# Retention heads: decay products ahead of the lo parts, gate weight sums in halves, and the gate's last products swapped round the first values

## The chip, the cores and the metric

The kernel runs on one core of a Trainium2 chip. The metric is the device time of one execution in microseconds (us), as a median of several executions. The engines are TensorE (PE, matmuls; PEld is its weight load), VectorE (DVE), ScalarE (ACT), GpSimd (POOL) and SyncE (SP), which issues the DMAs here. Each engine works through its own row of instructions in order and waits there for others by semaphores.

## What is computed

One decoder layer over 512 positions and 16 meta tokens at width 1024: two mixers on the same normalised input, gated retention (4 heads) and stick-breaking attention (16 heads), then an output product and a SwiGLU feed-forward part (FFN). Only retention matters for the change. Cut to that, with the chunked sums written as one:

```python
q = rotary(heads(rq)) * 256 ** -0.5      # 4 heads, 256 wide
k = rotary(heads(rk))                    # 16 meta rows ahead of the 512
v, gate = heads(rv), rg                  # 512 wide a head
scores = (q @ k.T) * decay               # decay[i, j] = g**(i-j) for i >= j, else 0
y = head_groupnorm(scores @ v)           # (y - mean) * rsqrt(var + 1e-5), per row
y_ret = (silu(gate) * y) @ w_ret_out
```

## The kernel before

**Numbers and products.** fp32 operands are carried as two parts: `split` (L99) has ACT copy a tile into the hi part, and `lo_of` (L96) has DVE subtract it from the source to give the lo part. Every product is three matmuls (hi by hi, hi by lo, lo by hi), all issued through `mm` (L90). So nearly every PE row of the profile says L90, every hi part L99 and every lo part L96, and tiles are told apart by name: `wh`/`wl` are weights' hi and lo parts, `qk` the parts of rotated q and k (later also of the transposed output), `sh`/`sl` those of the scores, `smt` those of the meta tokens' scores, `tm` a decay product, `ub` the combined results of seven products, `raw` a loaded weight, `st` a sum of weight quarters.

**Seven products.** The gate, the values and FFN multiply by a Strassen-Winograd scheme. `tok_quarters` (L255-283) loads a weight in two pieces, forms four sums of its quarters on POOL (x, y and two in place, L277-280), and splits seven units in the order a11, a12, s2, s3, s1, s4, a22. `seven` (L285-307) makes the seven products in PSUM banks and combines them on DVE into `ub` (L296, L299, L302, L307). The products are numbered 0 to 6: product 5 uses s4 and product 6 uses a22; both land in one two-bank tile. `after` is a hook in which `rv_proj` puts the meta tokens' part.

**Banks.** PSUM is handed out from three pools with two buffers each: `bank_p` (512 columns), `bank_b` (512 columns) and `bank_a` (1024 columns). Scores, y and the transposes take `bank_b`. `wraw` holds two loaded weight pieces; `rt` has three buffers for rotation temporaries, decay products and y.

**A retention head** (loop from L1045): `ret_qk` projects and rotates q, projects k in two halves of 128 rows into two `bank_a` tiles, and rotates k (`rotate`, L915-929: L921 to L923 make the first half and L925 to L928 the second, each followed by a split). `tok_quarters` loads and splits the gate's weights. `ret_scores` (L955-983) makes 6 matmuls for the meta tokens' scores, then 6 for each of four blocks j (512, 384, 256 and 128 columns), multiplies each by the decay (L966 for meta, L978 for the blocks) and splits it. `ret_gate` (L1007) makes the gate's seven products and a silu. `ret_pv` (L985) makes the four row blocks y0 to y3, each with mean, variance, reciprocal root (`rstd_of`, a power on POOL at L143) and the product with the gate; `ret_T` transposes; `rv_proj(h+1)` projects the next head's values; `ret_out` multiplies by the output weight.

**Who sets the order.** The kernel is written for a framework whose scheduler orders each engine's row. It may put instructions in another order than the code has them where their data allows, except that `keep` returns matmuls marked to keep program order while `pinned[0]` is true. In the retention heads of the kernel before it is false: the scheduler puts the gate's products between k's projection and the scores, and the scores in between them.

Of the kernel before, what the change touches and what calls it, by code (L numbers as in the profile page):

```python
# [10 lines left out]
F32 = mybir.dt.float32  # L11
# [5 lines left out]
P = 128  # L17
# [17 lines left out]
def hybrid_block(  # L35
# [219 lines left out]
    def tok_quarters(src, sums=None):  # L255

        raws = []
        for i in range(2):
            raw = wraw.tile([P, KH, 512], F32, tag="raw", name="raw")
            nc.sync.dma_start(raw, src[KH * P * i : KH * P * (i + 1), :].rearrange("(k p) c -> p k c", p=P))  # L260
            raws.append(raw)
        A11, A21 = raws[0][:, :, 0:256], raws[0][:, :, 256:]
        A12, A22 = raws[1][:, :, 0:256], raws[1][:, :, 256:]
        u = {}
        u["a11"] = wun_split(A11)
        u["a12"] = wun_split(A12)
        if sums is None:
            u["a22"] = wun_split(A22)
            nc.gpsimd.tensor_tensor(A22, A21, A22, op=ALU.add)
            nc.gpsimd.tensor_tensor(A21, A11, A21, op=ALU.subtract)  # L270
            nc.gpsimd.tensor_tensor(A11, A22, A11, op=ALU.subtract)
            nc.gpsimd.tensor_tensor(A12, A12, A11, op=ALU.subtract)
            u["s2"], u["s3"], u["s1"], u["s4"] = [wun_split(a) for a in (A11, A21, A22, A12)]
            return u
        x = sums.tile([P, KH, 256], F32, tag="st", name="st")
        y = sums.tile([P, KH, 256], F32, tag="st", name="st")
        nc.gpsimd.tensor_tensor(y, A11, A21, op=ALU.subtract)  # L277
        nc.gpsimd.tensor_tensor(A21, A21, A22, op=ALU.add)
        nc.gpsimd.tensor_tensor(x, A21, A11, op=ALU.subtract)  # L279
        nc.gpsimd.tensor_tensor(A12, A12, x, op=ALU.subtract)  # L280
        u["s2"], u["s3"], u["s1"] = wun_split(x), wun_split(y), wun_split(A21)
        u["s4"], u["a22"] = wun_split(A12), wun_split(A22)
        return u

    def seven(product, bank1, bank2, ub, after=lambda n: None):  # L285


        n = ub.shape[-1]
        p1 = bank1()
        product(0, p1)  # L290
        nc.scalar.activation(ub[:, 1, :], p1, AF.Copy)
        p = bank2()
        product(1, p[:, 0, :])
        after(1)
        product(2, p[:, 1, :])
        nc.vector.tensor_tensor(ub[:, 0:2, :], p, ub[:, 1:2, :].to_broadcast([P, 2, n]), op=ALU.add)  # L296
        p = bank1()
        product(3, p)
        nc.vector.tensor_tensor(ub[:, 2, :], p, ub[:, 1, :], op=ALU.add)  # L299
        p = bank1()  # L300
        product(4, p)
        nc.vector.tensor_tensor(ub[:, 1:4:2, :], p.rearrange("p (o n) -> p o n", o=1).to_broadcast([P, 2, n]), ub[:, 1:3, :], op=ALU.add)  # L302
        p = bank2()
        product(5, p[:, 0, :])
        product(6, p[:, 1, :])
        after(6)
        nc.vector.tensor_tensor(ub[:, 1:3, :], p, ub[:, 1:3, :], op=ALU.add)  # L307

    def feat_seven(u, tok, ub):
# [645 lines left out]
    def ret_scores(h, q, k):  # L955
        st = []
        dec = s4.tile([P, L], F32, tag="dec", name="dec", bufs=1)
        nc.sync.dma_start(dec, decay[h])
        pb = bank_b()
        n = 0  # L960
        for e in range(2):
            for a, b in ((0, 0), (0, 1), (1, 0)):
                mm(pb[:NM], k[e][a][:, 0:NM], q[e][b][:, :T], start=(n == 0), stop=(n == 5))
                n += 1
        tm = s4.tile([P, T], F32, tag="rt", name="tm", bufs=RT)
        nc.vector.tensor_tensor(tm[:NM], pb[:NM], dec[0:NM, NM:], op=ALU.mult)  # L966
        split(smt[0:16, :], smt[32:48, :], tm[:NM])
        nc.scalar.activation(smt[64:80, :], smt[0:16, :].bitcast(F32), AF.Copy)
        for j in range(NT):
            w = T - j * P  # L970
            pb = bank_b()
            n = 0
            for e in range(2):
                for a, b in ((0, 0), (0, 1), (1, 0)):
                    mm(pb[:, :w], k[e][a][:, NM + j * P : NM + (j + 1) * P], q[e][b][:, j * P : T], start=(n == 0), stop=(n == 5))
                    n += 1
            tm = s4.tile([P, T], F32, tag="rt", name="tm", bufs=RT)
            nc.vector.tensor_tensor(tm[:, :w], pb[:, :w], dec[:, :w], op=ALU.mult)  # L978
            sh = s4.tile([P, w], F32R, tag=f"sh{j}", name="sh", bufs=1)
            sl = s4.tile([P, w], F32R, tag=f"sl{j}", name="sl", bufs=1)  # L980
            split(sh, sl, tm[:, :w])
            st.append((sh, sl))
        return st

    def ret_pv(h, st, vts, us, gts):  # L985

        for i in range(NT):
            y = bank_b()
            mm(y, smt[:, i * P : (i + 1) * P], rvm, start=True, stop=False)
            for j in range(i + 1):  # L990
                cs = slice((i - j) * P, (i - j + 1) * P)
                sh, sl = st[j]
                vh, vl = vts[j]
                mm(y, sh[:, cs], vh, start=False, stop=False)
                mm(y, sh[:, cs], vl, start=False, stop=False)
                mm(y, sl[:, cs], vh, start=False, stop=(j == i))
            stt = s4.tile([P, 6], F32, tag="bn", name="bn")
            nc.vector.bn_stats(stt, y)
            mv = s4.tile([P, 2], F32, tag="mv", name="mv")
            nc.vector.bn_aggr(mv, stt)  # L1000
            rs = s4.tile([P, 1], F32, tag="rs", name="rs")
            rstd_of(rs, mv[:, 1:2], 1e-5, 1.0)
            yn = s4.tile([P, DV], F32, tag="rt", name="yn", bufs=RT)
            nc.vector.tensor_scalar(yn, y, mv[:, 0:1], rs, op0=ALU.subtract, op1=ALU.mult)
            nc.vector.tensor_tensor(gts[i], yn, gts[i], op=ALU.mult)

    def ret_gate(u):  # L1007
        ub = s4.tile([P, 4, 512], F32, tag="ub", name="ub", bufs=1)
        tok_seven(u, tokens, ub)
        g = s4.tile([P, NT, DV], F32, tag="g", name="g", bufs=1)  # L1010
        for q in range(4):
            c, t = q // 2, q % 2
            dst = g[:, 2 * t : 2 * t + 2, 256 * c : 256 * (c + 1)]
            nc.scalar.activation(dst, ub[:, q, :].rearrange("p (a b) -> p a b", a=2), AF.Silu)
        return [g[:, i, :] for i in range(NT)]

    def ret_T(gts):
        yT = []
# [27 lines left out]
    for h in range(RH):  # L1046
        q, k = ret_qk(h)
        us = tok_quarters(w_in[:, O_RG + DV * h : O_RG + DV * (h + 1)], s4)
        st = ret_scores(h, q, k)
        gts = ret_gate(us)  # L1050
        ret_pv(h, st, vts, us, gts)
        yT = ret_T(gts)
        if h + 1 < RH:
            vts = rv_proj(h + 1)
            ret_out(h, yT, first if h == 0 else add)
        else:

            gall = [s4.tile([P, 4, T], F32, tag=t, name="ga", bufs=1) for t in ("vh", "vl")]
            ga = [gall[f // 4][:, f % 4, :] for f in range(KD)]
            base = []  # L1060
            for f in range(0, KD, 2):
                mb = s4.tile([P, 2, T], F32, tag="st", name="mb")
                nc.sync.dma_start(mb, mS_d[:, f : f + 2, :])
                base += [mb[:, 0, :], mb[:, 1, :]]

                def gate(f):
                    nc.vector.tensor_tensor(acc[:, f, :], acc[:, f, :], ga[f], op=ALU.mult)
                    nc.vector.tensor_tensor(acc[:, f, :], acc[:, f, :], base[f], op=ALU.add)

                for e in range(f, f + 2):  # L1070
                    if e < NGE:
                        nc.sync.dma_start(ga[e], ga_d[:, e, :])
                    else:
                        (u,) = feat_units(w_in[:, O_GA + P * e : O_GA + P * (e + 1)])
                        ps = bank_p()
                        feat_mm(ps, u, xtok, ltok)
                        nc.scalar.activation(ga[e], ps, AF.Sigmoid)
                    gate(e)

            def merge(f, ps):  # L1080
                t = s4.tile([P, L], F32, tag="rt", name="mg", bufs=RT)[:, :T]
                nc.vector.tensor_tensor(t, ps, ga[f], op=ALU.mult)
                nc.vector.tensor_tensor(t, t, acc[:, f, :], op=ALU.add)
                split(hT[:, f, NM:], hL[:, f, NM:], t)

            ret_out(h, yT, merge)
# [225 lines left out]
```

## Time and profile before

| | us |
|---|---|
| median of 3 executions (1228.42 to 1229.15) | 1228.53 |
| the profiled execution | 1228.66 |
| its span | 1226.9 |
| mean granted TensorE clock | 0.993 |

In the span the retention heads run from about 360 to 820 us; in the four heads k's last product ends at 406.8, 515.6, 625.2 and 734.0. FFN's first products run from 875 to 1100, and its output follows to 1215. A timeline row has the start, the duration, the engine, the line, the operation, out<-in with shapes, the count, and in brackets the idle time before it with what ended that. A row by windows has start and end, the length, then the busy time and count of PE, PEld, DVE, ACT and POOL, the granted PE clock as a share of full speed, the share of the DMA engines, and GB/s.

### The profile page before, as it was taken

Reading aid. Unit: us, or ns where it says so; the run is one execution under the profiler, and the core shown is the slowest. Engines: PE = TensorE matmul, PEld = TensorE weight load, DVE = VectorE, ACT = ScalarE, POOL = GpSimd, SP = SyncE. Lnnn points to the kernel's source line nnn. Section 1 sums busy time; section 2 is a strip of 40 time slices with the busy share of each in tenths; the row PEclk is TensorE's granted clock in tenths of the full one; section 3 lists DMA queues with packets and bytes.
Section 4 is the critical chain, followed back from the end, with each engine's and each line's share of the span. In section 5 each row is a group of like instructions: output and inputs, shape, how many; then the busy total and the mean of one; then the engine's idle time right before and its main releaser. Section 6 shows DMA issues by size and latency. Waiting matters only on the chain.

```text
span 1226.9 us, 18829 instructions
## 1 busy us (share of the span) xinstructions
PE 1172.9 (96%) x7597; PEld 1063.2 (87%) x7597; DVE 884.1 (72%) x1133; ACT 532.8 (43%) x869; POOL 390.9 (32%) x425
## 2 busy tenths in 40 slices
PE   7999999889999999989999999999989999999997
PEld 7888888788889988988898899778979999998886
DVE  5588888887537885586678657776799999984333
ACT  5476666655423435342342424334354444443221
POOL 2037767553033210230212020000555666730000
PEclk9999999999999999999999999999999999999999
DMA  6331112114633213122321424424223333343211
GB/s 191 87 95 44 52 52 62 43 44 154 224 130 104 70 59 122 46 97 70 106 70 44 137 69 147 136 88 153 70 69 104 104 104 104 104 158 134 80 58 68
DMA packets 94503, 118.23 MB, mean 96 GB/s; under 512 B 2489, under 2 KB 71105, under 8 KB 94417
## 3 DMA queue, kind: packets, MB, share of 16 engines
q1 hardware_dynamic: 93984, 115.98, 29.2%
q8 instruction: 59, 0.97, 0.3%
q10 hardware_dynamic: 432, 1.07, 0.3%
q14 instruction: 28, 0.22, 0.1%
HBM read 109.96 MB, written 7.08 MB: 95 GB/s over the span
## 4 chain that ended last, share of the span: by engine, by line
PE 70%; DVE 14%; issue 4%; ACT 3%; POOL 3%; DMA 2%; DVEq 0%; POOLq 0%; ACTq 0%; SPq 0%
PE pp L90 30%; PE pb L90 18%; PE pa L90 16%; PE pc L90 4%; DVE wl L96 3%; DVE sm L645 2%; DVE sp L646 2%; PE pb L93 2%; DVE sl L96 1%; ACT wh L99 1%; POOL mg L654 1%; DMA raw<-in_w_in_dram 1%; DVE kl L96 1%; DMA raw<-in_w_sb_out_dram 1%; DMA raw<-in_w_ffn_in_dram 1%
## 5 line engine op out<-in xcount | busy, mean ns | idle before, releaser
L96 DVE TENSOR_TENSOR wl<-raw,wh 128x1024 fp32r<-128x1024 f32 (+1 forms) x202 | 275.2, 1371 | 81.1 <-ACT wh L99 77.8
L99 ACT ACTIVATE wh<-raw 128x1024 fp32r<-128x1024 f32 (+1 forms) x202 | 201.2, 1007 | 255.2 <-PE pp L90 85.5
L90 PE MATMUL pp<-hT,wh 128*128 128x512 f32 (+2 forms) x308 | 109.3, 355 | 13.0 <-DVE qb L96 8.1
L90 PE MATMUL pp<-hL,wh 128*128 128x512 f32 (+2 forms) x308 | 104.0, 338 | 0.0
L90 PE MATMUL pp<-hT,wl 128*128 128x512 f32 (+2 forms) x308 | 103.9, 337 | 0.0
L90 PE MATMUL pp<-qk,wh 128*128 128x512 f32 x256 | 83.1, 399 | 2.0 <-ACT qk L99 1.7
L96 DVE TENSOR_TENSOR wl<-st,wh 128x1024 fp32r<-128x1024 f32 x54 | 80.2, 1490 | 6.6 <-ACT wh L99 6.5
L90 PE MATMUL pp<-wh,hT 128*128 128x256 f32 (+1 forms) x240 | 78.0, 326 | 2.1 <-DVE kl L96 1.4
L90 PE MATMUL pp<-wh,hL 128*128 128x256 f32 (+1 forms) x240 | 76.6, 319 | 0.8 <-DVE ss L142 0.8
L90 PEld LDWEIGHTS pp<-hT,wh 128*128 128x128 f32 x308 | 58.6, 190 | 20.2 <-issue 10.2
L90 PE MATMUL pp<-wl,hT 128*128 128x256 f32 (+1 forms) x240 | 76.1, 317 | 0.0
L99 ACT ACTIVATE wh<-st 128x1024 fp32r<-128x1024 f32 x54 | 55.8, 1054 | 44.5 <-POOL st L279 17.1
L277 POOL TENSOR_TENSOR st<-raw 128x1024 f32<-128x1024 f32 x7 | 17.3, 2470 | 166.6 <-DMA raw<-in_w_in_dram 166.6
L143 POOL TENSOR_TENSOR rs<-rs,nhalf 128x1 f32<-128x1 f32 x20 | 12.2, 612 | 181.4 <-DVE rs L142 181.4
L654 POOL CAST mg<-sp 128x16 fp32r<-128x16 f32 x64 | 31.1, 486 | 109.4 <-DVE sp L646 53.6
L90 PEld LDWEIGHTS pp<-hT,wl 128*128 128x128 f32 x308 | 58.5, 190 | 6.1
L90 PEld LDWEIGHTS pp<-hL,wh 128*128 128x128 f32 x308 | 58.8, 191 | 3.8
L645 DVE TENSOR_TENSOR_SCAN sm<-sm,mask 128x528 f32<-128x528 f32 (+1 forms) x64 | 59.7, 946 | 2.6 <-ACT sm L641 2.1
L90 PE MATMUL pa<-hL,wh 128*128 128x264 f32 (+1 forms) x192 | 61.6, 321 | 0.0
L90 PE MATMUL pa<-hT,wl 128*128 128x264 f32 (+1 forms) x192 | 61.6, 321 | 0.0
L90 PE MATMUL pa<-hT,wh 128*128 128x264 f32 (+1 forms) x192 | 61.6, 321 | 0.0
L90 PEld LDWEIGHTS pp<-qk,wh 128*128 128x128 f32 x256 | 47.6, 188 | 13.4 <-ACT qk L99 2.4
(341 smaller groups left out, 3855.2 us busy)
## 6 DMA issues: line engine op xcount, KB each, us to landing
raw<-in_w_in_dram SPq DMA_DIRECT2D x31, 1024.0 KB, 5.0
raw<-in_w_ffn_in_dram SPq DMA_DIRECT2D x22, 1024.0 KB, 5.1
raw<-in_w_in_dram SPq DMA_DIRECT2D x26, 512.0 KB, 4.2
raw<-in_w_ffn_out_dram SPq DMA_DIRECT2D x11, 1024.0 KB, 5.0
raw<-in_w_ret_out_dram SPq DMA_DIRECT2D x8, 1024.0 KB, 5.1
raw<-in_w_sb_out_dram SPq DMA_DIRECT2D x4, 1024.0 KB, 7.4
raw<-in_w_out_dram SPq DMA_DIRECT2D x4, 1024.0 KB, 5.1
ysb<-in_x_dram SPq DMA_DIRECT2D x4, 512.0 KB, 8.9
```

Of the source, the lines that this page charges most:

```text
L90: return keep(nc.tensor.matmul(*args, **kw))
L93: return keep(nc.tensor.transpose(dst, src, idn))
L96: nc.vector.tensor_tensor(lo, src, hi.bitcast(F32), op=ALU.subtract)
L99: ins = nc.scalar.activation(hi, src, AF.Copy)
L143: nc.gpsimd.tensor_tensor(dst, dst, nhalf[:n], op=ALU.pow)
L277: nc.gpsimd.tensor_tensor(y, A11, A21, op=ALU.subtract)
L645: nc.vector.tensor_tensor_scan(rev, rev, mask[:, r0:][:, ::-1], 0.0, op0=ALU.mult, op1=ALU.max)
L646: nc.vector.tensor_tensor(sp, sp, sm[:, r0 + 1 : L + 1], op=ALU.mult)
L654: nc.gpsimd.tensor_copy(g[:, i, 0:NM], att[i][:, 0:NM])
```

## The change

There are four edits.

1. `ret_scores` issues all decay products (now L985) ahead of the blocks' splits; the meta scores' split comes at block 2, and block 3's decay product is put into the free end of block 1's `tm`.
2. `ret_gate` sets `pinned[0]` around the gate's seven products and, through the hook, puts y0's matmuls (`ret_y`) behind product 6; `ret_pv` makes y1 to y3.
3. `seven` makes product 6 ahead of product 5, wherever it is used, and `tok_quarters` splits a22 ahead of s4.
4. `tok_quarters` makes each of the four sums in two halves (the gate of each head, and the values of heads 1 to 3).

```diff
 tok_quarters:
-        nc.gpsimd.tensor_tensor(y, A11, A21, op=ALU.subtract)
-        nc.gpsimd.tensor_tensor(A21, A21, A22, op=ALU.add)
-        nc.gpsimd.tensor_tensor(x, A21, A11, op=ALU.subtract)
-        nc.gpsimd.tensor_tensor(A12, A12, x, op=ALU.subtract)
+        for d, p, q, op in ((y, A11, A21, ALU.subtract), (A21, A21, A22, ALU.add), (x, A21, A11, ALU.subtract), (A12, A12, x, ALU.subtract)):
+            for k in range(0, KH, 2):
+                nc.gpsimd.tensor_tensor(d[:, k : k + 2], p[:, k : k + 2], q[:, k : k + 2], op=op)
         u["s2"], u["s3"], u["s1"] = wun_split(x), wun_split(y), wun_split(A21)
-        u["s4"], u["a22"] = wun_split(A12), wun_split(A22)
+        u["a22"], u["s4"] = wun_split(A22), wun_split(A12)
...
 seven:
-        product(5, p[:, 0, :])
         product(6, p[:, 1, :])
         after(6)
+        product(5, p[:, 0, :])
...
 ret_scores:
-        split(smt[0:16, :], smt[32:48, :], tm[:NM])
-        nc.scalar.activation(smt[64:80, :], smt[0:16, :].bitcast(F32), AF.Copy)
+        tms = {}
         for j in range(NT):
+            if j == 2:
+                split(smt[0:16, :], smt[32:48, :], tmm[:NM])
+                nc.scalar.activation(smt[64:80, :], smt[0:16, :].bitcast(F32), AF.Copy)
...
-            tm = s4.tile([P, T], F32, tag="rt", name="tm", bufs=RT)
-            nc.vector.tensor_tensor(tm[:, :w], pb[:, :w], dec[:, :w], op=ALU.mult)
+            if j < 3:
+                tm = s4.tile([P, T], F32, tag="rt", name="tm", bufs=RT)
+                tms[j] = tm[:, :w]
+            if j == 1:
+                tms[3] = tm[:, w : w + P]
+            nc.vector.tensor_tensor(tms[j], pb[:, :w], dec[:, :w], op=ALU.mult)
+        for j in range(NT):
+            w = T - j * P
...
-            split(sh, sl, tm[:, :w])
+            split(sh, sl, tms[j])
...
 ret_gate:
+        def after(n):
+            if n == 6:
+                y0.append(ret_y(0, st, vts))
+
+        pinned[0] = True
+        tok_seven(u, tokens, ub, after=after)
+        pinned[0] = False
```

The first place is PE's row in head 0, from the last matmul of k's projection (`pa_4486`). Here `pp_4658` is the gate's first product, `qk_4409` and `qk_4410` are q's first half in hi and lo, `qk_4535` and `qk_4536` k's first half, and `pb_4593` the meta scores. Before, the gate's matmuls follow k directly, and the scores come in among them later:

```order
L90 MATMUL pa_4486<-hT_83,wl_4434 128x264
L90 MATMUL pp_4658<-wh_4557,hL_84 128x256
L90 MATMUL pp_4658<-wh_4557,hT_83 128x256
...
L90 MATMUL pa_4684<-wh_4561,hT_83 128x256
L90 MATMUL pb_4593<-qk_4409,qk_4535 16x512
L90 MATMUL pb_4593<-qk_4410,qk_4535 16x512
L90 MATMUL pb_4605<-qk_4409,qk_4535 128x512
L90 MATMUL pb_4605<-qk_4410,qk_4535 128x512
L90 MATMUL pa_4684<-wl_4562,hT_83 128x256
```

Now the scores follow k directly (`pb_4597` meta, `pb_4606` block 0; `qk_4411`, `qk_4412` are q's second half, `qk_4537`, `qk_4538` k's), and the gate's first product, `pp_4661`, comes after the last block:

```order
L90 MATMUL pa_4486<-hT_83,wl_4434 128x264
L90 MATMUL pb_4597<-qk_4409,qk_4535 16x512
L90 MATMUL pb_4597<-qk_4410,qk_4535 16x512
L90 MATMUL pb_4606<-qk_4409,qk_4535 128x512
L90 MATMUL pb_4606<-qk_4410,qk_4535 128x512
L90 MATMUL pb_4597<-qk_4409,qk_4536 16x512
L90 MATMUL pb_4606<-qk_4409,qk_4536 128x512
L90 MATMUL pb_4597<-qk_4411,qk_4537 16x512
...
L90 MATMUL pb_4636<-qk_4411,qk_4538 128x128
L90 MATMUL pp_4661<-wh_4557,hT_83 128x256
```

Between k's projection and the scores there is no matmul any more that can run without the rotated k. All four heads read alike here.

The second place is DVE's row in head 0, at the same point of the work. Before, two decay products, parts of weights (`wl`) and parts of scores (`sl`) alternate, with the fourth decay product (128 columns) behind them:

```order
L96 TENSOR_TENSOR sl_4615<-tm_4612,sh_4614 128x512
L978 TENSOR_TENSOR tm_4625<-pb_4618,dec_4591 128x384
L978 TENSOR_TENSOR tm_4638<-pb_4631,dec_4591 128x256
L96 TENSOR_TENSOR wl_4964<-raw_4957,wh_4963 128x1024
L96 TENSOR_TENSOR sl_4628<-tm_4625,sh_4627 128x384
L96 TENSOR_TENSOR sl_4641<-tm_4638,sh_4640 128x256
L978 TENSOR_TENSOR tm_4651<-pb_4644,dec_4591 128x128
L96 TENSOR_TENSOR wl_4974<-st_4967,wh_4973 128x1024
```

Now the four decay products alternate with score parts alone, and the weights' parts come behind all of them:

```order
L966 TENSOR_TENSOR tm_4604<-pb_4597,dec_4595 16x512
L985 TENSOR_TENSOR tm_4613<-pb_4606,dec_4595 128x512
L96 TENSOR_TENSOR smt_4060<-tm_4604,smt_4060 16x512
L985 TENSOR_TENSOR tm_4622<-pb_4615,dec_4595 128x384
L96 TENSOR_TENSOR sl_4645<-tm_4613,sh_4644 128x512
L985 TENSOR_TENSOR tm_4634<-pb_4627,dec_4595 128x256
L96 TENSOR_TENSOR sl_4649<-tm_4622,sh_4648 128x384
L985 TENSOR_TENSOR tm_4622<-pb_4636,dec_4595 128x128
L96 TENSOR_TENSOR sl_4653<-tm_4634,sh_4652 128x256
L96 TENSOR_TENSOR sl_4657<-tm_4622,sh_4656 128x128
L96 TENSOR_TENSOR wl_4588<-raw_4555,wh_4587 128x1024
L96 TENSOR_TENSOR wl_4592<-raw_4555,wh_4591 128x1024
```

The lo parts of the last two gate units (`wl_4588`, `wl_4592`) moved from ahead of the scores' decay products to behind the scores' last part.

More of the change, by code (lines that the diff above doesn't have):

```diff
@@ L964, in ret_scores @@
                 n += 1
-        tm = s4.tile([P, T], F32, tag="rt", name="tm", bufs=RT)
-        nc.vector.tensor_tensor(tm[:NM], pb[:NM], dec[0:NM, NM:], op=ALU.mult)
-        split(smt[0:16, :], smt[32:48, :], tm[:NM])
-        nc.scalar.activation(smt[64:80, :], smt[0:16, :].bitcast(F32), AF.Copy)
+        tmm = s4.tile([P, T], F32, tag="rt", name="tm", bufs=RT)
+        nc.vector.tensor_tensor(tmm[:NM], pb[:NM], dec[0:NM, NM:], op=ALU.mult)
+        tms = {}
         for j in range(NT):
+            if j == 2:
+                split(smt[0:16, :], smt[32:48, :], tmm[:NM])
+                nc.scalar.activation(smt[64:80, :], smt[0:16, :].bitcast(F32), AF.Copy)
             w = T - j * P
@@ L976, in ret_scores, with ret_y, ret_pv @@
                     n += 1
-            tm = s4.tile([P, T], F32, tag="rt", name="tm", bufs=RT)
-            nc.vector.tensor_tensor(tm[:, :w], pb[:, :w], dec[:, :w], op=ALU.mult)
+            if j < 3:
[6 more added lines that the diff above has]
+            w = T - j * P
             sh = s4.tile([P, w], F32R, tag=f"sh{j}", name="sh", bufs=1)
             sl = s4.tile([P, w], F32R, tag=f"sl{j}", name="sl", bufs=1)
-            split(sh, sl, tm[:, :w])
+            split(sh, sl, tms[j])
             st.append((sh, sl))
         return st
-    def ret_pv(h, st, vts, us, gts):
-        for i in range(NT):
[L988 to L996, printed above, removed]
+    def ret_y(i, st, vts):
+        y = bank_b()
+        mm(y, smt[:, i * P : (i + 1) * P], rvm, start=True, stop=False)
+        for j in range(i + 1):
+            cs = slice((i - j) * P, (i - j + 1) * P)
+            sh, sl = st[j]
+            vh, vl = vts[j]
+            mm(y, sh[:, cs], vh, start=False, stop=False)
+            mm(y, sh[:, cs], vl, start=False, stop=False)
+            mm(y, sl[:, cs], vh, start=False, stop=(j == i))
+        return y
+    def ret_pv(y0, st, vts, gts):
+        for i in range(NT):
+            y = ret_y(i, st, vts) if i else y0
             stt = s4.tile([P, 6], F32, tag="bn", name="bn")
@@ L1005, in ret_pv, with ret_gate @@
             nc.vector.tensor_tensor(gts[i], yn, gts[i], op=ALU.mult)
-    def ret_gate(u):
+    def ret_gate(u, st, vts):
         ub = s4.tile([P, 4, 512], F32, tag="ub", name="ub", bufs=1)
-        tok_seven(u, tokens, ub)
+        y0 = []
+        def after(n):
[4 more added lines that the diff above has]
+        pinned[0] = False
         g = s4.tile([P, NT, DV], F32, tag="g", name="g", bufs=1)
@@ L1014, in ret_gate @@
             nc.scalar.activation(dst, ub[:, q, :].rearrange("p (a b) -> p a b", a=2), AF.Silu)
-        return [g[:, i, :] for i in range(NT)]
+        return [g[:, i, :] for i in range(NT)], y0[0]
     def ret_T(gts):
@@ L1049, in hybrid_block @@
         st = ret_scores(h, q, k)
-        gts = ret_gate(us)
-        ret_pv(h, st, vts, us, gts)
+        gts, y0 = ret_gate(us, st, vts)
+        ret_pv(y0, st, vts, gts)
         yT = ret_T(gts)
```

## The prediction

> **What bounds the kernel now.** The page comes first. TensorE (PE) is busy for 96% of the span, so in most stages a microsecond is gained or lost only where PE waits or where its clock falls.
>
> ```profile
> span 1226.9 us, 18829 instructions
> PE 1172.9 (96%) x7597; PEld 1063.2 (87%) x7597; DVE 884.1 (72%) x1133; ACT 532.8 (43%) x869; POOL 390.9 (32%) x425
> ```
>
> The change lies mostly in the four retention heads, so the second view is PE's waits from 300 to 880 us: total, times, longest. Only two belong to the edited code, the scores' decay products and the transposed output's parts.
>
> ```profile
> PE pb L90 <- DVE tm L978: 7.6, 3, 3.2
> PE pp L90 <- ACT qk L99: 1.7, 3, 0.6
> ```
>
> The third view is a table by stretch (length; busy PE, weight loads, DVE, ACT, POOL; clock; DMA). While k of head 0 is rotated (around 407 to 414), PE is busy all the time: gate products cover the rotation. The 2.24 us wait before 432.98 is one of the three on line 978, and about 1.5 us behind it the granted clock is 0.50 for 3.41 us. Two later heads show the same.
>
> ```profile
> 400.00:430.00 30.00, 30.00 (x240) 29.20 (x239) 24.27 (x26) 12.84 (x18) 8.38 (x4) 1.00 0.22 72
> 430.74:432.98 2.24, 0.00 (x1) 0.03 (x1) 2.24 (x3) 1.12 (x3) 1.60 (x1) 1.00 0.00 0
> 434.52:437.93 3.41, 3.41 (x18) 3.41 (x18) 3.41 (x5) 0.63 (x1) 0.00 (x0) 0.50 0.11 42
> 543.75:547.16 3.41, 3.41 (x18) 3.41 (x17) 3.41 (x5) 0.77 (x2) 0.00 (x0) 0.50 0.25 74
> 652.97:656.39 3.42, 3.42 (x18) 3.42 (x17) 3.42 (x5) 0.63 (x1) 0.00 (x0) 0.50 0.16 57
> ```
>
> ```profile
> 542.74 0.47 PE L90 MATMUL pb<-rvm,smt 80*128 80x512 f32 x1 [3.17 <-DVE tm L978]
> 651.41 0.47 PE L90 MATMUL pb<-rvm,smt 80*128 80x512 f32 x1 [2.24 <-DVE tm L978]
> ```
>
> **What goes.** The fourth decay product and its lo part come late, because DVE takes weight splits and lo parts between the decay products. Now six of the gate's seven products stand between the scores and y0: 144 matmuls at 0.125 (240 in 30.00 us above), 18 us of PE work. So these waits go: 2.24 + 3.17 + 2.24 = 7.6. The clock drops that follow them should go too: each does in 3.41 us what takes 1.7 at full clock, three make 5.1. Sum removed: **12.7 us**. Head 3 has neither.
>
> **What comes: k's rotation in the open.** With the gate's products held in written order behind the scores, directly behind k's last matmul stand matmuls that need the rotated k. The timeline of DVE and ACT gives the chain (start, duration, instruction):
>
> ```profile
> 406.86 0.71 DVE L922 TENSOR_TENSOR rt<-pa,sinT 128x528 f32<-128x528 f32 x1 [3.47 <-PE pa L90]
> 407.49 0.70 DVE L926 TENSOR_TENSOR rt<-pa,sinT 128x528 f32<-128x528 f32 x1
> 408.10 0.70 DVE L923 TENSOR_TENSOR rt<-rt 128x528 f32<-128x528 f32 x1
> 408.72 1.22 DVE L96 TENSOR_TENSOR wl<-raw,wh 128x1024 fp32r<-128x1024 f32 x1
> 409.86 0.70 DVE L927 TENSOR_TENSOR rt<-pa,cosT 128x528 f32<-128x528 f32 x1
> 411.61 0.70 DVE L96 TENSOR_TENSOR qk<-rt,qk 128x528 fp32r<-128x528 f32 x1
> 412.22 0.70 DVE L928 TENSOR_TENSOR rt<-rt 128x528 f32<-128x528 f32 x1
> 413.63 0.71 DVE L96 TENSOR_TENSOR qk<-rt,qk 128x528 fp32r<-128x528 f32 x1 [0.71 <-ACT qk L99]
> ```
>
> ```profile
> 410.06 0.64 ACT L99 ACTIVATE qk<-rt 128x528 fp32r<-128x528 f32 x1
> ```
>
> Let zero be the start of L922. L923 ends at 1.94 (408.80). Before, ACT was still at two other jobs; these are no longer ahead of it, so the first hi part is done at 2.6 and PE starts at about 2.7. On DVE one weight lo part (1.22) still stands there, but the second of before is gone; stepping down the rows, which overlap by 0.08, the first lo part ends at 4.31, L928 at 4.92, ACT's second hi part at 5.6, the second lo part at 6.35.
>
> PE has 12 matmuls of 512 columns for that time (the meta tokens' scores and those of block 0), in two halves:
>
> ```profile
> 412.85 1.09 PE L90 MATMUL pb<-qk 128*16 128x512 f32 x4
> 421.44 1.92 PE L90 MATMUL pb<-qk 128*128 128x384 f32 x12
> 418.54 0.67 DVE L966 TENSOR_TENSOR tm<-pb,dec 16x512 f32<-16x512 f32 x1
> 424.02 0.88 DVE L978 TENSOR_TENSOR tm<-pb,dec 128x384 f32<-128x384 f32 x2
> ```
>
> Four take 1.09 with their modelled tail, so I use 0.23 each. Four run from 2.7, two from 4.45, four from 5.7, two from 6.6; the last is done near 7.05. Of that 12 x 0.232 = 2.8 is work: **4.3 idle**. Then blocks 1 and 3 wait for a bank: there are two, and the first is free only after L966 (0.67), which starts when the meta scores are done. I put 0.75 there, and 0.15 for block 3, since blocks 1 and 2 (1.92 us) cover most of block 0's decay product: 0.9. So **5.2 idle a head, 20.8 in four**. Without the bank waits 17.2. Behind the waiting scores stands everything else of PE, the gate's products first. On DVE the gate's last two weight lo parts and the sum of line 296 now stand behind the score lo parts; the fifth product is the first to need them, some 9 us of PE work later, so I cost that at nothing; if it fails, PE waits there for parts of 1.22 each.
>
> **The halves and POOL.** When POOL's instruction and a DVE one with two SBUF inputs meet, both are long: the same lo part took 1.22 above and 2.46 here.
>
> ```profile
> 425.00 2.46 DVE L96 TENSOR_TENSOR wl<-raw,wh 128x1024 fp32r<-128x1024 f32 x1
> 427.38 5.25 DVE L96 TENSOR_TENSOR sl<-tm,sh 128x384 fp32r<-128x384 f32 x2
> 423.88 2.49 POOL L278 TENSOR_TENSOR raw<-raw 128x1024 f32<-128x1024 f32 x1 [6.34 <-DMA raw<-in_w_in_dram]
> 426.45 3.26 POOL L279 TENSOR_TENSOR st<-raw 128x1024 f32<-128x1024 f32 x1
> 410.01 9.03 SPq L260 DMA_DIRECT2D raw<-in_w_in_dram  x2
> L230 POOL TENSOR_TENSOR st<-raw 128x512 f32<-128x512 f32 x20 | 27.7, 1384 | 52.1 <-DVE wl L96 26.1 <-DMA raw<-in_w_ffn_in_dram 19.2 <-DVE ub L296 6.8
> ```
>
> A half costs 1.38 on average, two halves 2.8 against 2.49 to 3.26 for a whole: nothing, or a few tenths of POOL, which waits mostly. But the next values' sums can start about 8 us after zero (issue at 410.01 and the landing), at the decay products and lo parts that free banks: 0 to 0.9 in each of heads 0 to 2, I take 0.45: **1.3**. The three lo parts that took up to 5.25 for two now lie under the gate's products.
>
> **Clock.** The new idle is broken: 2.7 in one piece, then pieces under 1. At 2.24 the drop came; one longer wait had none, and the 5 us behind it ran at 1.00:
>
> ```profile
> 896.58 0.38 PE L90 MATMUL pp<-tl,wh 128*128 128x256 f32 x1 [2.56 <-DVE tl L96]
> 897.00:902.00 5.00, 3.46 (x29) 3.26 (x28) 5.00 (x5) 1.06 (x1) 4.20 (x2) 1.00 0.02 3
> ```
>
> So between 0 and 1.7 a head; part of a slow stretch would fall on idle PE. I take 0.5: **2.0**. The Trainium skill ("TensorE: Matmul & The Clock Gate", Part 1: The HAM clock gate) has the clock fall only after an idle window of about 3.4 us. By that rule no head would lose anything here and the sum would be 1238.5; the 0.50 behind a wait of 2.24 contradicts it, so I keep my term.
>
> **Small edits.** The transposes' parts wait 0.58 three times now; the head's products then follow the last transposes, whose bank needs both parts (0.60 and 0.69), again about 0.7 three times: +0.4, from nothing to +2.1.
>
> ```profile
> 461.23 0.73 PE L90 MATMUL pp<-qk,wh 128*128 128x512 f32 x2 [0.58 <-ACT qk L99]
> 464.47 0.60 ACT L99 ACTIVATE qk<-pb 128x512 fp32r<-128x512 f32 x1 [1.23 <-PE pb L93]
> 465.10 0.69 DVE L96 TENSOR_TENSOR qk<-pb,qk 128x512 fp32r<-128x512 f32 x1 [1.14 <-ACT qk L99]
> ```
>
> The last two products change places in FFN and values as well. There a22's parts, needed earlier now, are made well ahead: 0, at most 1.5. The decay's DMA now goes ahead of a values load on SP's queue, where PE does not wait for either: 0.
>
> **Sum.** 20.8 + 1.3 + 2.0 + 0.4 - 12.7 = +11.8. The profiled execution took 1228.66 (1.76 beyond its span), 0.13 over the median of 1228.53. Forecast: **1240.5**. Least: 17.2 - 12.7 - 1.7 (transposes gain) = +2.8, 1231.5. Most: 20.8 + 2.7 + 6.8 + 2.1 + 1.5 - 12.7 = +21.2, 1249.9.
>
> **Rivals.** *Hidden rotation (faster).* If PE is idle only until the first hi part, 2.7 a head, since q's and meta's matmuls or longer banks fill the rest: 10.8 - 12.7 - 1.7 = -3.6, about 1225.1. It decides below 3.6 idle a head. For it: 7 us of DVE work were hidden before. Against: 12 matmuls of 0.23 cannot fill 7 us, and the order leaves PE nothing else.
>
> *Even.* Idle of 3.2 to 3.6 a head, no clock loss: 1228.7. What a measurement can tell from no change is 0.2%, 2.5 us.
>
> *Late sums (slower yet).* In heads 0 to 2, y0's reciprocal root (POOL L143, behind the sums) comes only after the next values' eight half sums; a bank of y0 stays taken and y2 waits. The second load of these sums waits for the gate's last lo part; landing near 23, six halves of 1.38 end at 31, root, y0's two DVE passes and the queue ahead of them free the bank at about 35. PE wants it at about 36: scores done at 10.4, six products 18, y0 0.5, the last product 3, y1 1.6, the values' first product 3 (estimates from the rows above). A margin of 1.4 us is within one long POOL-DVE meeting (1.24). Price up to 3 us in three heads: 1249.5.
>
> **How the numbers follow.** Forecast 0.68, late sums 0.16, hidden 0.09, even 0.07. The range takes the forecast's bounds and most of late sums: 1231.0 to 1250.0; left out are hidden and even (0.16). Faster 0.09, same 0.07, slower 0.84.
>
> **What would show it.** In the profile after: PE's wait on L978 gone; a new wait of scores on ACT and DVE qk near 2.7 and of several tenths, four times, with 4 to 5.5 us idle behind each k projection, and PE idle up by some 13 us before the clock; no 0.50 stretches at 434, 543, 653, perhaps some 3 us behind each rotation. Wrong if PE is busy through the rotation, if waits behind it pass 7 us, or if y2 waits for a bank.

## The result and the profile after

The changed kernel takes 1248.68 us (median), 1.0161 times the kernel before, with a 95% interval of 1.0145 to 1.0177. Slower was forecast, with 1240.5 and a range of 1231.0 to 1250.0; the time is 8 us above the forecast and near the upper end. A second measurement of the same kernel, beside other runs of the kernel before, gave 1.0147 (1.0123 to 1.0171). One of the four executions of the first measurement took 1443.66 at a granted clock of 0.75; the ratio leaves it out, and the other three took 1247.64 to 1248.80.

The profiled execution took 1247.64. Its span is 17.8 us longer, and PE is busy 5.6 us longer:

```profile
span 1244.7 us, 18880 instructions
...
PE 1178.5 (95%) x7597; PEld 1061.6 (85%) x7597; DVE 878.7 (71%) x1133; ACT 535.2 (43%) x869; POOL 401.3 (32%) x453
```

PE's waits from 300 to 880 us. The waits on line 978 are gone. In their place stand eight waits on k's hi parts, four on the meta scores' decay product, and one kind that was not forecast, on line 927. Of the five waits on lo parts, two are k's (0.45 and 0.59), and three of 0.62 stand behind the transposed output, where three of 0.58 on ACT stood:

```profile
PE pb L90 <- ACT qk L99: 11.9, 8, 2.7
PE pb L90 <- DVE qk L96: 2.9, 5, 0.6
PE pb L90 <- DVE tm L966: 2.0, 4, 0.5
PE pa L90 <- DVE rt L927: 1.6, 2, 0.8
...
PE pb L90 <- DVE tm L985: 0.7, 1, 0.7
```

The timeline of head 0 shows the gap. DVE's row gives zero (the start of L922), PE's rows the scores behind it: the first wait is 2.71, and the gate's first product (`pp`) starts 11.56 us after zero. In head 3, where no next values' sums run on POOL, it starts 10.44 after zero.

```profile
408.83 0.71 DVE L922 TENSOR_TENSOR rt<-pa,sinT 128x528 f32<-128x528 f32 x1 [2.66 <-PE pa L90]
...
744.05 0.71 DVE L922 TENSOR_TENSOR rt<-pa,sinT 128x528 f32<-128x528 f32 x1 [2.74 <-PE pa L90]
```

```profile
411.50 2.73 PE L90 MATMUL pb<-qk 128*16 128x512 f32 x6 [2.71 <-ACT qk L99]
414.48 1.90 PE L90 MATMUL pb<-qk 128*16 128x512 f32 x6 [0.26 <-ACT qk L99]
416.91 2.02 PE L90 MATMUL pb<-qk 128*128 128x384 f32 x12 [0.53 <-DVE tm L966]
419.67 0.89 PE L90 MATMUL pb<-qk 128*128 128x128 f32 x6 [0.73 <-DVE tm L985]
420.39 0.33 PE L90 MATMUL pp<-wh,hT 128*128 128x256 f32 x1
...
754.49 0.33 PE L90 MATMUL pp<-wh,hT 128*128 128x256 f32 x1
```

The stretches at half clock (sixth number behind the length, 0.50) have moved: four lie behind the rotations, one for each head, and one of 10.24 us in the first FFN products, which the kernel before did not have in its profile. One more of 3.41 stands ahead of the heads in each of the two traces, at 73.90 here and at 185.35 before.

```profile
411.82:415.24 3.42, 3.12 (x8) 1.28 (x7) 2.64 (x5) 0.64 (x1) 0.00 (x0) 0.50 0.62 176
524.46:531.29 6.83, 5.78 (x15) 3.14 (x14) 4.17 (x7) 2.20 (x4) 2.01 (x2) 0.50 0.47 154
637.10:640.52 3.42, 3.12 (x8) 1.45 (x8) 1.19 (x2) 0.64 (x1) 0.00 (x0) 0.50 0.86 295
746.33:749.74 3.41, 2.78 (x7) 1.15 (x8) 2.70 (x5) 0.97 (x2) 0.00 (x0) 0.50 0.35 102
913.58:923.82 10.24, 8.22 (x35) 7.63 (x36) 10.24 (x9) 5.54 (x8) 6.03 (x3) 0.50 0.21 63
```

Where the 17.8 us lie: the retention heads with what follows them, up to the first transposes of the mixed output, are one row by windows in each trace, of before and of after. They are 13.95 us longer; 2.2 lie ahead of them and 1.7 behind.

```profile
358.76:850.48 491.72, 481.80 (x3010) 432.01 (x3009) 343.13 (x442) 181.38 (x252) 86.45 (x49) 0.99 0.31 100
```

```profile
360.94:866.61 505.67, 486.46 (x3011) 429.58 (x3010) 335.13 (x442) 183.91 (x252) 98.96 (x77) 0.98 0.30 97
```

### The profile page after: what moved, and what is told of

It is laid out like the page before. It is cut to its first block, busy times and chain, and to the rows that moved or that the text cites. A ratio compares the mean times of both kernels' runs of the same rounds, so it can differ in the third digit from the quotient of the medians.

```text
span 1244.7 us, 18880 instructions
## 1 busy us (share of the span) xinstructions
PE 1178.5 (95%) x7597; PEld 1061.6 (85%) x7597; DVE 878.7 (71%) x1133; ACT 535.2 (43%) x869; POOL 401.3 (32%) x453
## 4 chain that ended last, share of the span: by engine, by line
PE 69%; DVE 14%; issue 4%; POOL 3%; DMA 3%; ACT 2%; DVEq 0%; POOLq 0%; ACTq 0%; SPq 0%
PE pp L90 29%; PE pb L90 19%; PE pa L90 16%; PE pc L90 4%; DVE wl L96 3%; DVE sm L645 2%; DVE sp L646 2%; DMA raw<-in_w_in_dram 2%; PE pb L93 2%; POOL mg L654 1%; ACT wh L99 1%; DVE kl L96 1%; DMA raw<-in_w_sb_out_dram 1%; DVE al L96 1%; POOL mg L655 1%
## 5 line engine op out<-in xcount | busy, mean ns | idle before, releaser
L96 DVE TENSOR_TENSOR wl<-raw,wh 128x1024 fp32r<-128x1024 f32 (+1 forms) x202 | 269.2, 1342 | 89.8 <-ACT wh L99 89.1
L280 POOL TENSOR_TENSOR st<-raw 128x512 f32<-128x512 f32 x28 | 39.8, 1441 | 166.6 <-DMA raw<-in_w_in_dram 166.6
L96 DVE TENSOR_TENSOR wl<-st,wh 128x1024 fp32r<-128x1024 f32 x54 | 84.2, 1564 | 9.8 <-ACT wh L99 9.7
L90 PE MATMUL pp<-qk,wh 128*128 128x512 f32 x256 | 80.3, 394 | 0.0
L90 PE MATMUL pp<-wh,hL 128*128 128x256 f32 (+1 forms) x240 | 73.7, 308 | 0.8 <-DVE ss L142 0.8
L90 PE MATMUL pp<-wl,hT 128*128 128x256 f32 (+1 forms) x240 | 73.4, 306 | 0.0
```

Of the source, the lines that this page charges most:

```text
L90: return keep(nc.tensor.matmul(*args, **kw))
L96: nc.vector.tensor_tensor(lo, src, hi.bitcast(F32), op=ALU.subtract)
L280: nc.gpsimd.tensor_tensor(d[:, k : k + 2], p[:, k : k + 2], q[:, k : k + 2], op=op)
```

## The experiments

Each ratio is to runs of the kernel before that were made beside it (medians 1226.3 to 1228.6), so ratios are compared rather than times.

**Pinning taken out, and pinning alone.** Theory A is that of the prediction: the pinned gate lays k's rotation open. Theory B blames the other edits. The first kernel is the changed one without the two lines, the second is the kernel before with only these:

```diff
 ret_gate:
-        pinned[0] = True
         tok_seven(u, tokens, ub, after=after)
-        pinned[0] = False
```

> The changed kernel without the pinning of the gate's seven products; all else of the change stays. Theory A (the pinning costs: k's rotation lies in the open, about 23 us of idle and slow PE in four heads): the scheduler puts gate products between k and the scores again, PE has no wait of 2.7 us behind k, and the time falls from 1248.7 to 1221 to 1231, the lower end if decay products first also removes the waits of y0. Theory B (the half sums, the a22-s4 order or y0's place cost the time): it stays above 1240.

Measured: 1225.15, ratio 0.9990 (0.9975 to 1.0006): all of the loss is gone, and no measurable gain is left.

> The kernel before with one edit: the gate's seven products are pinned. Theory A: waits of 2.7 us behind k in all four heads, waits of y0 on the fourth decay product gone, time 1238 to 1250, much as the whole change. Theory B: within 3 us of 1228.8, since none of the edits that it blames is in.

Measured: 1247.19, ratio 1.0173 (1.0150 to 1.0195), as much as the whole change. Its waits on k are those of the changed kernel, with two left on a decay product:

```profile
PE pb L90 <- ACT qk L99: 12.3, 8, 2.7
PE pb L90 <- DVE qk L96: 2.4, 4, 0.6
PE pb L90 <- DVE tm L978: 2.1, 2, 1.9
```

So theory A holds and B falls as the cause of the whole. But pinning alone costs 21 us, twice what the prediction's terms give for it (20.8 + 2.0 - 12.7), so the other edits were tried one by one too.

**PE kept busy in the gap.** Idle and half clock are mixed in the changed kernel. Matmuls that nothing uses fill the first wait, behind k's pinned products:

```diff
 ret_qk:
+        pinned[0] = True
         for e in range(2):
...
+        fill = bank_p()
+        for i in range(22):
+            mm(fill[:, :256], hT[:, i % KD, 0:P], hT[:, i % KD, NM : NM + 256], start=(i == 0), stop=(i == 21))
+        pinned[0] = False
         k = [(qk_tile(), qk_tile()) for _ in range(2)]
```

> The changed kernel with k's projection pinned too and 22 more matmuls of 256 columns (about 2.7 us) behind it in each head, whose result nothing uses: PE is busy while it would wait for k's first hi part, and no useful work is moved. It separates idle from the lower clock behind it. If the clock drop is paid beside the idle: the half-clock stretches in the heads go and 6 to 8 us with them, 1241 to 1243. If the slow stretch falls mostly on time in which the scores wait anyway: the stretches go, but only 0 to 3 us, 1245.5 to 1249.

Measured: 1240.36, ratio 1.0118 (1.0097 to 1.0139). The half-clock stretches in the heads are gone. The changed kernel measured again, against the same two lines of figures:

> The changed kernel itself once more, on the chip and beside the runs of the kernel before that the next three have. Both theories: 1.4 to 1.8% slower than the kernel before. Its five half-clock stretches in the heads come again behind the waits of 2.7 us if they follow from these waits; if they were chance, they do not.

Measured: 1245.21, ratio 1.0147 (1.0123 to 1.0171), with the stretches back behind every rotation. By the ratios the fill wins 3.6 to 5.3 us against the two measurements, between the two expectations; its interval overlaps that of the second a little. The traces place a part of it: from L922 in head 0 to L922 in head 3, two rows by windows each, the filled kernel takes 334.33 us and the changed one 335.83 in its second trace (335.22 in its first), so 0.3 to 0.5 a head.

```profile
404.38:627.59 223.21, 215.43 (x1422) 194.51 (x1421) 144.96 (x183) 82.19 (x110) 53.86 (x40) 1.00 0.23 79
627.59:738.71 111.12, 107.71 (x712) 97.21 (x711) 74.78 (x96) 38.36 (x51) 26.74 (x20) 1.00 0.27 88
```

```profile
405.58:629.34 223.76, 212.78 (x1376) 190.33 (x1376) 144.49 (x182) 82.07 (x110) 53.83 (x40) 0.98 0.24 78
629.34:741.41 112.07, 107.54 (x688) 96.12 (x688) 73.07 (x96) 38.33 (x51) 26.75 (x20) 0.97 0.27 87
```

In the gap the slow clock falls mostly on time in which the scores would have waited. The waits show it: from L922 to the gate's first product PE waits 15.6 and 16.5 us in the four heads of the two traces of the changed kernel, and 10.0 in the filled one, which with four fills of 2.7 makes 20.8. So the lower clock stretches matmuls into 4 to 5 us of waiting. The rest of the difference lies outside the heads, and why is not shown.

**Halves alone.** The kernel before with the sums' loop of the diff and nothing else:

> The kernel before with one edit: the four sums of weight quarters in halves. Theory A: no measurable difference, within 2.5 us. Theory B (the halves delay sums, splits or y0's reciprocal root): 4 to 9 us slower.

Measured: 1217.64, ratio 0.9922 (0.9903 to 0.9941). Neither expectation: the halves win 9 us. DVE's rows in head 0 show how. Beside whole sums, the prediction quoted 2.46 for a weight's lo part and 5.25 for two lo parts of scores; the fourth decay product follows them:

```profile
432.55 0.28 DVE L978 TENSOR_TENSOR tm<-pb,dec 128x128 f32<-128x128 f32 x1
```

With halves, and POOL's first two of them:

```profile
425.91 1.53 DVE L96 TENSOR_TENSOR wl<-raw,wh 128x1024 fp32r<-128x1024 f32 x1
427.36 3.06 DVE L96 TENSOR_TENSOR sl<-tm,sh 128x384 fp32r<-128x384 f32 x2
430.34 0.28 DVE L977 TENSOR_TENSOR tm<-pb,dec 128x128 f32<-128x128 f32 x1
```

```profile
423.34 3.01 POOL L279 TENSOR_TENSOR raw<-raw 128x512 f32<-128x512 f32 x2 [4.05 <-DMA raw<-in_w_in_dram]
```

Both weight lo parts end about their undisturbed 1.2 us behind the end of POOL's instruction: 427.46 behind 426.37 (423.88 + 2.49, both rows quoted in the prediction), and 427.44 behind 426.35 here. So in these rows a DVE subtraction that meets a POOL sum waits for that instruction to end, and a shorter instruction is a shorter wait. The decay products beside the same sums, which have one input in PSUM, are not lengthened (0.88 for two in both traces). Counted from L922 (406.86 there; 407.63 here, where it is L921) the fourth decay product comes at 22.7 instead of 25.7. The waits of y0 on it are gone (0.9 in each of three heads is left, on the gate's sum in line 301), and so are the three stretches at half clock. The Trainium skill ("GPSIMD Engine Reference", 1. Specifications) says that POOL shares its SBUF interfaces with VectorE, with contention where a DVE instruction has two SBUF inputs. These rows agree, and show that here the wait lasts to the end of POOL's instruction, so its cost goes with the length of that.

**Decay products first, alone, and the swap alone.** The kernel before with the diff's `ret_scores`:

> The kernel before with one edit: all decay products ahead of the blocks' splits. The gate stays unpinned. Theory A: the waits of y0 on the fourth decay product (7.6 us in three) go with this edit alone, and the half-clock stretches behind them; since other waits can take their place, 0 to 8 us are won. Rival (the waits need the gate between scores and y0): the waits stay, within 2 us of the kernel before.

Measured: 1225.51, ratio 0.9989 (0.9976 to 1.0003). The rival was right that the waits of y0 stay:

```profile
PE pb L90 <- DVE tm L985: 6.5, 3, 2.2
```

But this run does not show that an earlier decay product would not help. Without the pinning the scheduler puts DVE's row back into the order of the kernel before: in heads 0 to 2 the fourth decay product still comes behind the same lo parts, beside the same whole sums, as in head 0:

```profile
427.76 5.26 DVE L96 TENSOR_TENSOR sl<-tm,sh 128x384 fp32r<-128x384 f32 x2
432.94 0.28 DVE L985 TENSOR_TENSOR tm<-pb,dec 128x128 f32<-128x128 f32 x1
```

The kernel before with product 6 ahead of 5 and a22 split ahead of s4:

> The kernel before with one edit: product 6 ahead of product 5 and a22 split ahead of s4. The halves alone gave 0.992 of the kernel before, but halves, swap and decay products first together (the changed kernel without the pinning) only 0.999. If the swap takes the gain back (new waits at the transposes' parts and at the combined result of products 5 and 6): 4 to 9 us slower than the kernel before. If it is the decay products first, together with the halves: within 2.5 us.

Measured: 1235.62, ratio 1.0066 (1.0050 to 1.0081). The swap costs 7 to 8 us. Its waits, and the place in head 0:

```profile
PE pp L90 <- ACT qk L99: 4.2, 3, 1.4
PE pb L93 <- DVE qk L96: 1.9, 3, 0.6
```

```profile
462.28 0.73 PE L90 MATMUL pp<-qk,wh 128*128 128x512 f32 x2 [1.41 <-ACT qk L99]
463.66 0.66 PE L93 MATMUL pb<-ident,g 128*128 128x128 f32 x4 [0.64 <-DVE qk L96]
```

```profile
460.69 1.06 ACT L99 ACTIVATE wh<-raw 128x1024 fp32r<-128x1024 f32 x1 [4.94 <-PE pa L90]
461.65 1.07 ACT L99 ACTIVATE qk<-pb 128x512 fp32r<-128x512 f32 x2
```

The last weight unit's hi part (1.06) now stands on ACT right ahead of the transposed output's parts; PE waits 1.41 for these where it waited 0.58, and the next transposes wait 0.64 more. That is 4.4 of the 7 to 8 us; the profile also has more half clock than before's (3.41 us more in head 1, 3.41 behind these waits in head 2, 6.83 in FFN's first products), which lies beside the rest.

**Scores inside the gate's products.** If the gap is the cost, work put into it wins it back. The scores were issued behind the gate's second product, then behind its third, all pinned:

```diff
 ret_gate:
...
         def after(n):
+            if n == 1:
+                st.extend(ret_scores(h, q, k))
             if n == 6:
                 y0.append(ret_y(0, st, vts))
...
```

The scores behind the third product are issued in the same way through a second hook, behind `product(2)`.

> The changed kernel with one edit: the scores are issued inside the gate's products, behind the second one, all pinned, so that 48 matmuls (6 us) stand between k's projection and the scores, and five products (15 us) between the scores and y0. Theory A: rotation covered (2.7 us waits gone), y0's waits gone as well, so below the kernel before: 1214 to 1224. Theory B: the edits that it blames are all in, so above 1240.

Measured: 1226.87, ratio 1.0002 (0.9991 to 1.0014): the loss is gone, but the gain did not come. The first two waits are shorter and not gone:

```profile
PE pb L90 <- ACT qk L99: 4.3, 4, 1.1
PE pb L90 <- DVE qk L96: 2.8, 4, 0.7
```

> The changed kernel with the scores issued inside the gate's products behind the third one (72 matmuls, 9 us, between k and the scores; 12 us between the scores and y0), all pinned. With the scores behind the second product PE still waited 7 us for parts of k. Theory A: these waits shrink to 0 to 3 us in all, those of y0 stay away, no half-clock stretch in the heads: 4 to 10 us below the kernel before. If the lo parts of the gate's weights, which stand among k's rotation on DVE, are what is late, the waits only move to the later score matmuls: within 2.5 us of it.

Measured: 1216.96, ratio 0.9921 (0.9900 to 0.9942). With 9 us of products, PE has no wait on `qk` left, y0 has none either, and there is no half clock in the heads. Still, the kernel is no faster than the halves alone (0.9922). Two variants of it: products 5 and 6 in the old order, and whole sums.

> The kernel with the scores behind the gate's third product, halves and decay products first, but products 5 and 6 and the splits of s4 and a22 in the old order; y0 stands behind the gate's last product. With the swap it gave 0.992. If the swap costs: 0.986 to 0.990. If it costs nothing here: 0.990 to 0.994.

Measured: 1219.77, ratio 0.9930 (0.9918 to 0.9942): the swap costs nothing measurable here.

> The kernel with the scores behind the gate's third product, with whole sums again. If the halves win only by the waits of y0, and 12 us of gate products cover these here: 0.990 to 0.995 as with halves. If whole sums hold up DVE's lo parts where something waits for them: 0.996 to 1.003.

Measured: 1235.09, ratio 1.0050 (1.0036 to 1.0064), over the upper expectation. With whole sums PE waits for decay products again, now in the scores, for banks that the decay products hold:

```profile
PE pb L90 <- DVE tm L987: 6.1, 3, 2.1
PE pb L90 <- DVE tm L968: 4.5, 4, 1.4
```

**Whole sums in the changed kernel.**

> The changed kernel with whole sums again; the other three edits stay. If the halves win only by the waits of y0, which the pinning takes away anyway: within 2.5 us of the changed kernel, 1.3 to 1.8% over the kernel before. If shorter sums help DVE elsewhere too: over 2% slower than the kernel before.

Measured: 1251.20, ratio 1.0193 (1.0173 to 1.0213), 0.3 to 0.5% over the two measurements of the changed kernel and between the two expectations; its interval just touches that of the first (up to 1.0177). So the halves win 4 to 6 us there too, though the pinned gate has taken away the waits that they remove in the kernel before. Some 3 us of it stand in the gap: from L922 to the gate's first product the four heads take 48.98 with whole sums, 45.75 and 46.49 in the two traces of the changed kernel, and 49.4 with pinning alone, which has whole sums too.

The halves alone and the scores behind the gate's third product are the best versions that ran, both at 0.992.

## Why the prediction was right, and where it was not

- **k's rotation in the open: right in kind, place and size.** The first wait was put at 2.7 and is 2.70 or 2.71 in all four heads. The scores were to be done 10.4 after zero, plus 0.45 for POOL in heads 0 to 2 and 0.5 for the clock: 44.9 in four heads. From L922 to the gate's first product the heads take 11.56, 12.13, 11.62 and 10.44: 45.75. At full clock the filled kernel shows 20.8 of idle in the four heads (10.0 left and 10.8 filled), POOL's part in it; 20.8 and 1.3 were forecast. In the changed kernel PE waits 3.5 to 4.2 a head, partly below the 4 to 5.5 given as a sign, since slow matmuls fill the rest.
- **The terms beside it: two errors that partly cancel.** The filled kernel, without slow clock, takes 11.53, 11.48, 11.38 and 10.46. Head 3, where POOL makes no sums for next values, is as forecast (10.4). Heads 0 to 2 take 0.9 to 1.1 more, by a wait of 0.9 to 1.0 on a decay product (L990 there) that head 3 does not have; 0.45 was put for POOL, at most 0.9. The changed kernel's two traces take 0.9 and 1.6 more in all for the clock, where 2.0 was put.
- **The clock: right in its reason.** 0.5 a head was taken from a range of 0 to 1.7, so that it came so near the 0.2 to 0.5 measured is partly luck. The rule of the Trainium skill weighed in the prediction ("TensorE: Matmul & The Clock Gate", Part 1: The HAM clock gate), under which no head would have lost clock, is contradicted: each of the four rotations was followed by 0.50.
- **What goes: right.** The three waits of y0 (7.6) and the three stretches behind them are not in the profile after. The reason given for the late decay product, the lo parts that DVE takes ahead of it, was half of it: with the order kept and only the sums halved, the waits on it go as well.
- **Late sums: did not happen in the profile after.** No wait of y2 for a bank stands among its waits, and the second measurement has one of 0.46 in one head, where the rival had up to 3 in three. So the time near that rival's 1249.5 does not speak for it.
- **Missed in the heads: 1.6 us.** k's second half waits 0.84 and 0.72 for a bank that q's rotation holds (L927). With the 0.85 above this makes 2.45. The transposes' waits grew by 0.1 (three of 0.62 for three of 0.58) where +0.4 was put. Together that is about the 2.15 between the +11.8 forecast and the 13.95 of the heads' row.
- **Outside the heads: 3.9 us, not forecast, and not explained by the change.** 2.2 lie ahead of the heads, where the code is the same. The changed kernel's second trace reaches the heads at 357.98, earlier than the kernel before (358.76), its first at 360.94: this part differs between executions of one kernel. Windows of the clock have a share. The waits at 71.9 and 73.4 are 1.42 and 0.91 in both traces, yet only after has half clock behind them (73.90 to 77.32); it is 1.5 us behind from there to 182, and the kernel before loses 1.2 of that again by half clock of its own (185.35 to 188.76). Longer waits on DVE near 196 and 307 make the rest. Of the 1.7 behind the heads the cause is open. In FFN's first products the wait for `tl` is 2.88 where it was 2.56, and 10.24 us at half clock follow. All nine traces with products 5 and 6 swapped have 6.83 or 10.24 us of half clock there, the five without have none or 3.41; but the swap alone does not make the part behind the heads longer (374.3, and 376.4 in the kernel before).
- **The step that failed: "a half costs 1.38 on average, two halves 2.8 ... nothing, or a few tenths of POOL".** It priced the halves by POOL's own time, though the row beside it (2.46 against 1.22) shows that the time is DVE's. Alone they win 9 us, in the changed kernel 4 to 6, and with the scores behind the third product 1.3% (0.9921 against 1.0050). In the changed kernel part of this is hidden, because the pinned gate removes the same waits of y0.
- **"0" for the last two products' change of places holds only beside the pinned gate.** There the transposes' waits stay near 0.6 and, with the scores behind the third product, no cost is measurable; in the kernel before it costs 7 to 8. I looked for a22's parts and not for what moved behind them on ACT. The single effects of halves, swap and decay products first do nearly add up: -0.8, +0.7 and -0.1% against the -0.1% of the three together.

## What to carry to other kernels

When an order is pinned, look for what the scheduler had put into the gap: the work that hid a serial chain on other engines is gone, and the price is that chain's length to the first part, plus the waits for later parts and banks behind it. Look at the row that the scheduler made, too: an edit that reorders the code may leave the row as it was. Put the chain's users a full chain's length behind its start (9 us here, where 6 were not enough). Where two engines hold each other up, cut the instructions of the one that has time to spare: an engine with 32% busy can still set the pace by the length of one instruction.

## What the runs showed of the hardware

**The clock falls by windows, on little more than half a window of idle.** All stretches at half clock lie on a grid of 3.41 us that runs on through the execution. I cut each of the 14 traces (before, after and the twelve experiments, from 30 to 1205 us) into windows on that grid and summed PE's idle time in each, by the modelled ends of its matmuls. Of 4746 windows at full clock 53 were followed by one at half clock: all 44 with at least 1.84 us idle, none with less than 1.74, and between these 9 of 13. From half clock it went back to full only after windows with up to 0.65 us idle; it stayed with more, and three times with less (0.12, 0.55, 0.55). Two windows of the changed kernel, with PE busy 0.70 and 0.81 (2.7 and 2.6 idle), each ahead of a 0.50:

```profile
408.41:411.82 3.41, 0.70 (x6) 0.36 (x5) 2.99 (x4) 1.70 (x2) 0.00 (x0) 1.00 0.00 0
521.05:524.46 3.41, 0.81 (x4) 0.49 (x4) 3.41 (x5) 1.58 (x2) 0.00 (x0) 1.00 0.00 0
...
70.49:73.90 3.41, 1.08 (x8) 0.87 (x8) 3.33 (x6) 1.71 (x5) 1.08 (x4) 1.00 0.53 154
73.90:77.32 3.42, 3.42 (x18) 3.42 (x18) 3.36 (x7) 1.11 (x3) 1.30 (x4) 0.50 0.00 0
```

And four of the kernel before: the first two, with 1.87 and 1.85 idle, are followed by the half clock of the first and last of its three stretches in the heads, the other two, with 1.59 and 1.54, by full clock.

```profile
431.11:434.52 3.41, 1.54 (x9) 1.39 (x10) 3.41 (x4) 1.89 (x3) 1.23 (x1) 1.00 0.16 38
649.56:652.97 3.41, 1.56 (x9) 1.42 (x10) 3.41 (x4) 1.87 (x3) 1.22 (x1) 1.00 0.16 27
69.30:72.71 3.41, 1.82 (x13) 1.42 (x11) 2.88 (x5) 2.89 (x9) 1.85 (x7) 1.00 0.50 144
898.73:902.14 3.41, 1.87 (x16) 1.67 (x16) 3.41 (x4) 1.06 (x1) 3.41 (x3) 1.00 0.00 0
```

Between 1.74 and 1.84 either can follow: near 182 us the kernel before has a window with 1.81 idle and half clock behind it, and the changed kernel one with 1.79 and full clock behind it (1.00 in 186.54 to 189.95).

```profile
181.94:185.35 3.41, 1.60 (x14) 1.42 (x13) 3.33 (x6) 3.35 (x11) 3.20 (x7) 1.00 0.14 38
185.35:188.76 3.41, 3.41 (x18) 3.41 (x17) 3.40 (x6) 1.89 (x3) 1.74 (x4) 0.50 0.42 123
```

The two waits at 71.9 and 73.4 us fall into one window of after (2.33 idle, its row from 70.49 above) and are cut by a border in before (1.59). So a wait of 2 to 3 us may or may not cost 1.7 us more, by where the grid lies in that execution. The kernel before spread from 1222.5 to 1230.3 over the runs beside the experiments; that this is the same chance is likely and was not shown. This also explains the wait of 2.56 that the prediction found without a drop: a border cut it into 1.30 and 1.26.
